# A three-stage transformer kernel: one order of two splits swapped, three pacing rates and the depth of a read changed

## The chip, the cores and the metric

The kernel runs on one core of one Trainium2 chip. The time is the device time of one launch in microseconds (us); the comparison is between medians of several launches of each kernel. One launch of each kernel is also recorded by the hardware profiler; all rows below come from that launch of the kernel before.

## What is computed

Two transformer blocks on 256 tokens of width 2048, all in float32. The first is a convolution and neighbourhood attention block with an MLP. The second has latent attention, a gated unit and, last, a retrieval layer over 16,384 experts. Only this last layer, and the second product of the MLP, lie near the change:

```python
f = jnp.square(jax.nn.relu(h @ w_up[l])) @ w_down[l]        # first block, the MLP

def peer_ffn(h, w_pq, peer_keys, peer_u, peer_v):            # second block, the last layer
    q = jnp.einsum("bsd,dhk->bshk", h, w_pq).reshape(B, S, PEER_HEADS, 2, KEY_DIM)
    sub = jnp.einsum("bshpk,hpnk->bshpn", q, peer_keys).astype(jnp.float32)
    s, i = lax.top_k(sub, PEER_TOPK)
    cand = (s[..., 0, :, None] + s[..., 1, None, :]).reshape(B, S, PEER_HEADS, PEER_TOPK * PEER_TOPK)
    ...
    top_s, pos = lax.top_k(cand, PEER_TOPK)
    idx = jnp.take_along_axis(cidx, pos, axis=-1)
    gate = jax.nn.softmax(top_s, axis=-1).astype(h.dtype)
    ...
        u = jnp.take(peer_u, i_blk, axis=0)
        a = jax.nn.gelu(jnp.einsum("td,thkd->thk", x_blk, u)) * g_blk
        v = jnp.take(peer_v, i_blk, axis=0)
        return jnp.einsum("thk,thkd->td", a, v)
```

Most tokens do not gather their experts. The kernel computes gelu(h @ peer_u.T) for all experts, multiplies it by a table that holds the gate of a chosen expert and zero elsewhere, and multiplies the result by peer_v. For 64 of the 256 tokens the table is not used: their rows of peer_u and peer_v are gathered, two experts of each of the 64 tokens per gather, 64 gathers of each matrix.

## The kernel before

**Weight steps.** All weights stream through three 1 MB buffers (`raw`), loaded on SP's queue (L209). Half a buffer is one weight step. For each step ScalarE writes the rounded high part (`whi`, L131), VectorE the rest (`wlo`, L132), and TensorE multiplies both by activations that have been split in the same way (L264). There are four `whi`/`wlo` pairs, so a split may run three steps ahead of its matmuls (`LOOK`). There are 1,124 weight steps, numbered from 0.

**Order.** `Builder.run` writes the program by hand, step by step: first `prep`, which splits the weights of a step up to three ahead, and which asks SP for the next load when it has used up a buffer; then `jit`, which splits the activations of a step two ahead where these are made just in time (the MLP's second product, and the value passes below); then the matmuls of the step; then `tick`. Each engine executes its own instructions in this written order.

**Side work.** `tick` moves generators forward. Each generator is a list of small portions of work and has a rate, the portions that it gets per weight step (`Gen`, `acc`). A generator that is not done when its result is needed is drained: the whole rest is written at once at that place.

**The last layer.** From step 612 on the passes are U(0), U(1), U(2), U(3), V(0), U(4), V(1), U(5), V(2), U(6), V(3), U(7), then V(4 to 7) in one piece of 128 steps; each other pass has 32 steps. A U pass multiplies by an eighth of peer_u; after every eight steps a `turn` transposes the result (L1635, L1637) and puts its gelu into a ring of four eighths (`s_ra`, `s_rc`). A V pass multiplies a ring entry by an eighth of peer_v; its stationary operand `s_vj` is split from the ring two steps ahead. Beside the passes run, one after the other:
- `top_gen` (*the search*): the second top 16, all on VectorE (L1485 to L1489, L1542 to L1547). It begins after the lists of the first top 16; rate 1.0.
- `g_gen` (*the gates*): 24 portions. Each makes one-hot tables on VectorE (four instructions, L1674 to L1677), multiplies them on TensorE (L1687), copies the product on ScalarE (L1689, two instructions) and stores 0.5 MB to the DRAM tile `scratch` (L1690). Two sets of tables are used in turn. Rate 0.5.
- `sparse` (*the gathers*): 128 gathers of 1 MB each on GpSimd's queue into three buffers (L1592), one instruction of VectorE for each (L1607 for peer_u, L1609 for peer_v). Rates 0.48 in U passes, 0.30 in V passes.
- `r_gen(e)` (*the reads*): once pass U(e) is done and all gates are made, three reads of 0.5 MB from `scratch` on SP's queue into one buffer (`s_g`, L1698); each is followed, some ticks later, by a multiplication of a part of ring entry e on VectorE (L1704). `jit_V` drains `r_gen(e)` before it splits from entry e.

In this kernel the search lasts from step 612 (the lists end at 625) to step 682, the gates to step 733, the gathers from there to step 1091. V(0) begins at step 740. The reads for entry 0 begin after step 733 and are drained at step 738.

The names TensorE (PE), VectorE (DVE), ScalarE (ACT), GpSimd (POOL) and SyncE (SP) are used below with the short forms that rows of the profile have.

Of the kernel before, what the change touches and what calls it, by code (L numbers as in the profile page):

```python
# [18 lines left out]
JLOOK = 2  # L19
# [38 lines left out]
class Builder:  # L58
# [22 lines left out]
    def H(self, i, key, dt=FT):  # L81

        s, n = (i // 2, 4096) if i >= 8 else (10 + i, 2048)
        if self.halves.get(s, (None,))[0] != key:
            self.halves[s] = key, self.pool.tile([128, n], dt, name=f"s{s}_{key}", tag=f"s{s}")
        o = 2048 * (i % 2) if i >= 8 else 0
        return self.halves[s][1][:, o:o + 2048]
# [197 lines left out]
    def run(self):  # L285
        prepared = jitted = 0
        while prepared < LOOK:
            self.first.upto(prepared + 1)
            self.prep(prepared)
            prepared += 1  # L290
        for i, halves, blocks, behind in self.order():
            p = self.pieces[i]
            self.spare = p.spare
            for need in p.need:
                g, n, hs = (need + (None,))[:3] if isinstance(need, tuple) else (need, None, None)
                if blocks in (None, (0,)) and (hs is None and halves[0] == 0 or hs in halves):
                    g().drain() if n is None else g().upto(n)
            while self.may_prep(prepared, i, behind):
                self.prep(prepared)
                prepared += 1  # L300
            while jitted <= i + JLOOK:
                self.jit(jitted)
                jitted += 1
            self.mm(i, halves, blocks)
            if p.lag is None:
                if p.post:
                    p.post(p)
                self.tick()
            else:
                self.tick(0.5 if blocks is None else 0.25)  # L310
                if p.post:
                    p.post(p, halves) if blocks is None else p.post(p, halves, blocks)
        for g in self.gens:
            g.drain()
# [622 lines left out]
XLOOK = 2  # L937
ASIDE = (1, 3, 4, 5, 6, 7)

GATE_RATE = 0.5  # L940

SPARSE_RATE = (0.48, 0.30)
CONV_RATE = [1.7, 1.2]
NA_RATE = [1.0, 1.0]
CONV_POOL = (2, 3, 6, 7)
# [2 lines left out]
def phase3(b, C, W, gs, X, ident, transposes, residual, norm_of, stat2, act_pair, lhs_of, res_need, bcast, jits,  # L948
# [429 lines left out]
    def fuse():  # L1378
        for c in range(0, 16, 4):
            yield  # L1380
            yield
            t = [v3(H(4 + k, "h", FR)[:, :], 16)[:, c:c + 4] for k in range(2)]
            A.activation(t[0][:, :, 64:128], t[1][:, :, 0:64], AF.Copy)
# [32 lines left out]
    def Qp(n, h):  # L1416
        return H(6, "top")[:, (n % 2) * 1024 + h * 512:(n % 2) * 1024 + h * 512 + 512]
# [10 lines left out]
    def key_gen(n):  # L1428
        if n:
            gs["key", n - 1].drain()  # L1430
        for _ in transposes(lambda h: Qp(n, h), 0, evac_to(lambda: qT(n))):
            yield
        yield
        for h in range(2):
            p = b.bank()
            for i in range(4):
                PE.matmul(p[:, i * 128:i * 128 + 128], qT(n)[:, i, h * 128:h * 128 + 128], keys()[:, 4 * n + i],
                          start=True, stop=True)
            A.activation(SUB(h)[:, n * 512:n * 512 + 512], p[:, :], AF.Copy)
            yield  # L1440
        if n == 3:
            for h in range(2):
                b.dbg(f"sub.{h}", SUB(h)[:, :])
# [5 lines left out]
    def post_pq(n):  # L1449
        def f(p):  # L1450
            if n == 0:
                for h in range(2):
                    gs["res3", h].drain()
                norm_of(r3, ss3)
                nc.gpsimd.dma_start(H(16, "k")[:, :], d["keysT"])
                for r, lo in ((rd, 0), (rsp, 64)):
                    for o in (0, 64):
                        nc.gpsimd.dma_start(r[o:o + 64, :], r3[lo:lo + 64, 1:2])
                nc.gpsimd.dma_start(fold, d["fold"])
            for h in range(2):  # L1460
                A.activation(Qp(n, h), b.ps[p.banks[h][0]][:, :], AF.Copy, scale=r3[:, h:h + 1])
            gs["key", n] = b.start(key_gen(n))
            gs["lists", n] = b.start(lists_gen(n))
            if n == 2:
                gs["fuse"] = b.start(fuse())
            if n == 3:
                gs["top"] = b.start(top_gen(), 1.0)
        return f

    for n in range(4):  # L1470
# [25 lines left out]
    def lists_gen(n):  # L1496
        V16, I16, _, rep = found()
        while not (gs["key", n].done and (n == 0 or gs["lists", n - 1].done)):
            yield
        for h in range(2):  # L1500
            for m in range(4 * n, 4 * n + 4):
                o = (h * 16 + m) * 16
                top16(V16[:, o:o + 16], I16[:, o:o + 16], SUB(h)[:, m * 128:m * 128 + 128], rep[m % 2][:, :128])
                yield

    def top_gen():
# [13 lines left out]
        for h in range(2):  # L1520
# [52 lines left out]
            yield  # L1573
        gs["G"] = b.start(g_gen(), GATE_RATE)

# [41 lines left out]
    def ring(e, h):  # L1617

        j = e % 4
        return v3(H(14 + j // 2, "rc")[:, j % 2 * 1024:j % 2 * 1024 + 1024] if h else H(10 + j, "ra")[:, :], 16)  # L1620
# [20 lines left out]
    def post_U(n):  # L1641

        def f(p):
            if n and ("s", n - 1) in gs:
                gs["s", n - 1].drain()
            for h in range(2):
                A.activation(GT(h), b.ps[p.banks[h][0]][:, :], AF.Copy, scale=rd if h else r3[:, 0:1])
            gs["s", n] = b.start(turn(n))
            if n % 4 == 3:
                gs["R", n // 4] = b.start(r_gen(n // 4))  # L1650
        return f
# [5 lines left out]
    def g_gen():  # L1657
# [12 lines left out]
        for k in range(25):  # L1670
# [8 lines left out]
            if k:  # L1679
# [10 lines left out]
                nc.gpsimd.dma_start(b.scratch[k], out[k % 2])  # L1690
        gs["sp"] = b.start(sparse(), SPARSE_RATE[0])

    def r_gen(e):
        while not (gs["s", 4 * e + 3].done and "G" in gs and gs["G"].done and (e == 0 or gs["R", e - 1].done)):
            yield
        t = H(7, "g")[:, 1024:2048]
        for j in range(3):
            nc.sync.dma_start(t.rearrange("p (k m) -> p k m", k=8),  # L1698
                              b.scratch[8 * j:8 * j + 8, :, 128 * e:128 * e + 128].rearrange("k p m -> p k m"))
            yield  # L1700
            yield
            yield
            R = ring(e, j // 2)[:, :, j % 2 * 64:j % 2 * 64 + 64].rearrange("p n (k t) -> p k n t", k=8)
            V.tensor_tensor(R, R, t.rearrange("p (k n t) -> p k n t", k=8, n=16), op=OP.mult)  # L1704
            yield
# [82 lines left out]
    def pace(i):  # L1788
        if "sp" in gs:
            gs["sp"].rate = SPARSE_RATE[i]  # L1790
        return Gen(iter(()))
# [131 lines left out]
```

## Time and profile before

| what | value |
|---|---|
| median of 3 launches | 3282.93 us (3282.73 to 3294.15) |
| the profiled launch's own time | 3288.91 us |
| its span, first to last instruction | 3287.1 us |
| busy: PE, DVE, ACT, POOL | 96%, 69%, 53%, 15% |
| moved by DMA | 768.52 MB, mean 234 GB/s |
| U and V passes (from step 612) | from 1903.8 us of the span |

A busy share is the share of the span in which the engine executed something. Busy time of PE is modelled at its ends, so small gaps do not show. The span is cut into stretches below by weight steps: a stretch begins where ACT begins the `whi` split of its first step.

### The profile page before, as it was taken

How to read it: one execution, taken by the hardware profiler on the slowest of the kernel's cores; microseconds unless marked ns; L12 is line 12 of the kernel's file. 1: busy time of each engine (PE TensorE's matmuls, PEld its weight loads, DVE VectorE, ACT ScalarE, POOL GpSimd, SP SyncE). 2: the span in 40 equal slices, each digit the busy share in tenths (PEclk: the TensorE clock that was granted, in tenths of full speed). 3: DMA queues.
4: the chain of work that ended last, by engine and by line, in shares of the span. 5: the costliest groups of instructions: out<-in, count | busy, mean ns of one | idle time of the engine just before them, and what ended most of it. 6: DMA issues, size and time to landing. Idle time of an engine off the chain costs nothing. (4 is left out here: it accounts for less than half of the span.)

```text
span 3287.1 us, 37918 instructions
## 1 busy us (share of the span) xinstructions
PE 3164.6 (96%) x14264; PEld 2474.4 (75%) x14264; DVE 2271.0 (69%) x2847; ACT 1725.9 (53%) x2490; POOL 480.5 (15%) x372
## 2 busy tenths in 40 slices
PE   8799999999999999999999999997899999999998
PEld 6577778888888788877778877775676767677776
DVE  6996554444555555654565599885898989898985
ACT  5666554444444455455544555675444545455554
POOL 3861010000000010000000100001131313232310
PEclk9999999999999999999999999998999999999999
DMA  6345455555555545544455555676999999999974
GB/s 224 134 163 182 179 178 180 179 179 181 191 189 183 200 139 214 181 160 144 140 184 189 180 183 201 240 266 231 339 397 350 400 351 397 346 400 359 365 296 154
DMA packets 135240, 768.52 MB, mean 234 GB/s; under 512 B 13008, under 2 KB 38016, under 8 KB 47568
## 3 DMA queue, kind: packets, MB, share of 16 engines
q1 hardware_dynamic: 110000, 604.81, 50.9%
q0 software_dynamic: 24768, 160.25, 12.4%
q8 instruction: 111, 1.82, 0.2%
q10 hardware_dynamic: 288, 1.05, 0.1%
q14 instruction: 73, 0.60, 0.1%
HBM read 750.82 MB, written 14.68 MB: 233 GB/s over the span
## 5 line engine op out<-in xcount | busy, mean ns | idle before, releaser
L132 DVE TENSOR_TENSOR wlo<-raw,whi 128x1024 fp32r<-128x1024 f32 (+2 forms) x1101 | 1350.9, 1235 | 790.5 <-ACT whi L131 780.9
L131 ACT ACTIVATE whi<-raw 128x1024 fp32r<-128x1024 f32 (+2 forms) x1113 | 1167.1, 1053 | 1050.4 <-PE ps L264 840.1
L264 PE MATMUL ps<-whi,s_x 128*128 128x512 f32 (+2 forms) x2816 | 908.6, 398 | 10.6 <-ACT whi L131 6.2
L264 PEld LDWEIGHTS ps<-whi,s_x 128*128 128x128 f32 x2816 | 533.0, 190 | 137.3 <-issue 8.3
L264 PE MATMUL ps<-whi,s_h 128*128 128x512 f32 x1760 | 604.6, 400 | 0.0
L264 PE MATMUL ps<-whi,s_vj 128*128 128x512 f32 x1536 | 542.7, 408 | 59.2 <-DVE s_vj L132 35.8
L264 PE MATMUL ps<-wlo,s_x 128*128 128x512 f32 (+2 forms) x1408 | 556.0, 395 | 16.3 <-DVE wlo L132 16.2
L264 PE MATMUL ps<-wlo,s_h 128*128 128x512 f32 (+1 forms) x1136 | 449.5, 396 | 6.2 <-DVE wlo L132 6.2
L264 PEld LDWEIGHTS ps<-whi,s_vj 128*128 128x128 f32 x1536 | 294.3, 193 | 170.9 <-DVE s_vj L132 48.0
L264 PE MATMUL ps<-wlo,s_vj 128*128 128x512 f32 (+1 forms) x1024 | 410.6, 401 | 0.0
L264 PEld LDWEIGHTS ps<-whi,s_h 128*128 128x128 f32 x1760 | 331.4, 188 | 99.9
L264 PEld LDWEIGHTS ps<-wlo,s_x 128*128 128x128 f32 x1408 | 267.9, 190 | 80.7 <-DVE wlo L132 24.3
L264 PE MATMUL ps<-whi,s_fj 128*128 128x512 f32 x1024 | 324.6, 397 | 2.8 <-DVE s_fj L132 2.0
L264 PEld LDWEIGHTS ps<-whi,s_fj 128*128 128x128 f32 x1024 | 193.5, 189 | 51.5 <-DVE s_fj L132 2.5
L264 PEld LDWEIGHTS ps<-wlo,s_h 128*128 128x128 f32 (+1 forms) x1136 | 185.9, 164 | 56.4 <-DVE wlo L132 10.4
L264 PE MATMUL ps<-wlo,s_fj 128*128 128x512 f32 x512 | 203.6, 398 | 0.0
L264 PEld LDWEIGHTS ps<-wlo,s_vj 128*128 128x128 f32 (+1 forms) x1024 | 168.5, 165 | 46.4 <-issue 1.0
L132 POOL TENSOR_TENSOR s_head<-raw,s_head 128x1024 fp32r<-128x1024 f32 x6 | 17.5, 2934 | 895.8 <-ACT s_head L131 895.8
L517 POOL TENSOR_TENSOR s_conv<-s_conv,s_u 128x256 f32<-128x256 f32 x120 | 122.6, 1054 | 44.1 <-ACT s_u L516 43.6
L1592 POOL DMA_INDIRECT s_k<-in_v_rows,vec x43 | 91.3, 2123 | 201.7 <-DVE s_sp L1609 179.7
L264 PEld LDWEIGHTS ps<-wlo,s_fj 128*128 128x128 f32 x512 | 96.8, 189 | 22.6
L1609 DVE SCALAR_TENSOR_TENSOR s_sp<-s_k,misc,s_sp 128x2048 f32<-128x2048 f32 x43 | 100.8, 2345 | 2.1 <-DMA s_k<-in_v_rows,vec 2.1
(333 smaller groups left out, 2972.9 us busy)
## 6 DMA issues: line engine op xcount, KB each, us to landing
raw<-in_peer_u SPq DMA_DIRECT2D x128, 1024.0 KB, 5.8
raw<-in_peer_v SPq DMA_DIRECT2D x128, 1024.0 KB, 7.0
raw<-in_w_in SPq DMA_DIRECT2D x101, 1024.0 KB, 4.8
raw<-in_w_up SPq DMA_DIRECT2D x64, 1024.0 KB, 4.8
raw<-in_w_down SPq DMA_DIRECT2D x64, 1024.0 KB, 4.8
raw<-in_w_out SPq DMA_DIRECT2D x32, 1024.0 KB, 4.8
raw<-in_w_pq SPq DMA_DIRECT2D x16, 1024.0 KB, 4.8
scratch<-s_k POOLq DMA_DIRECT2D x24, 512.0 KB, 2.9
```

Source lines behind the costliest of these rows:

```text
L131: nc.scalar.activation(hi, src, AF.Copy)
L132: (engine or nc.vector).tensor_tensor(lo, src, hi.bitcast(FT), op=OP.subtract)
L264: nc.tensor.matmul(self.ps[p.banks[h][b]][:xs[q].shape[-1], :w], xs[q], (wl if q == 1 else wh)[:, s], start=p.first and c == 0 and q == 0, ...
L517: G.tensor_tensor(o, o, t, op=OP.add)
L1592: nc.gpsimd.indirect_dma_start(buf[g % 3], None, d["v_rows" if g // 64 else "u_rows"], at)
L1609: V.scalar_tensor_tensor(Y(), t, a, Y(), op0=OP.mult, op1=OP.add)
```

## The change

Four edits. The generator rates of the search (1.0 to 1.3) and of the gates (0.5 to 0.8) are raised, those of the gathers lowered (0.48 to 0.45 and 0.30 to 0.28). In `r_gen` there are five ticks instead of three between a read and the multiplication that uses it, for all entries but the first. In `run`, `jit` comes before `prep`, in every step of the program that has both.

```diff
@@ Builder.run
+            while jitted <= i + JLOOK:
+                self.jit(jitted)
+                jitted += 1
             while self.may_prep(prepared, i, behind):
                 self.prep(prepared)
                 prepared += 1
-            while jitted <= i + JLOOK:
-                self.jit(jitted)
-                jitted += 1
             self.mm(i, halves, blocks)
...
-GATE_RATE = 0.5
-
-SPARSE_RATE = (0.48, 0.30)
+GATE_RATE = 0.8
+
+SPARSE_RATE = (0.45, 0.28)
...
@@ post_pq
             if n == 3:
-                gs["top"] = b.start(top_gen(), 1.0)
+                gs["top"] = b.start(top_gen(), 1.3)
...
@@ r_gen
             nc.sync.dma_start(t.rearrange("p (k m) -> p k m", k=8),
                               b.scratch[8 * j:8 * j + 8, :, 128 * e:128 * e + 128].rearrange("k p m -> p k m"))
-            yield
-            yield
-            yield
+            for _ in range(5 if e else 3):
+                yield
             R = ring(e, j // 2)[:, :, j % 2 * 64:j % 2 * 64 + 64].rearrange("p n (k t) -> p k n t", k=8)
```

In the changed program the search ends at step 668, the gates at step 701, and the gathers run from step 701 to step 1070. The reads for entry 0 take steps 702 to 714, those for entry 1 steps 715 to 732, for entry 2 steps 733 to 750, for entry 3 steps 751 to 768; none is drained. The changed program has one line less, so L1704 is L1703 there. Where the programs differ is shown by their instructions in written order, at three places.

VectorE while the gates are made, before (`wlo` is a weight step's split; the four lines after it are one portion of the gates):

```order
L132 TENSOR_TENSOR wlo_81<-raw_75,whi_77 128x1024
L132 TENSOR_TENSOR wlo_82<-raw_73,whi_78 128x1024
L1674 TENSOR_TENSOR s_k<-s_g 128x1024
L1675 TENSOR_TENSOR s_k<-s_g 128x1024
L1676 TENSOR_TENSOR s_k<-s_k,s_g 128x1024
L1677 TENSOR_TENSOR s_k<-s_k,s_g 128x1024
L132 TENSOR_TENSOR wlo_83<-raw_73,whi_79 128x1024
L132 TENSOR_TENSOR wlo_80<-raw_74,whi_76 128x1024
```

and now:

```order
L132 TENSOR_TENSOR wlo_81<-raw_73,whi_77 128x1024
L1674 TENSOR_TENSOR s_k<-s_g 128x1024
L1675 TENSOR_TENSOR s_k<-s_g 128x1024
L1676 TENSOR_TENSOR s_k<-s_k,s_g 128x1024
L1677 TENSOR_TENSOR s_k<-s_k,s_g 128x1024
L132 TENSOR_TENSOR wlo_82<-raw_74,whi_78 128x1024
L1674 TENSOR_TENSOR s_gb<-s_g 128x1024
L1675 TENSOR_TENSOR s_gb<-s_g 128x1024
L1676 TENSOR_TENSOR s_gb<-s_gb,s_g 128x1024
```

A portion stands in four of five weight steps instead of in every second one.

VectorE where the reads for entry 0 are used, before (L1704 multiplies a ring entry by a read, L1587 belongs to the gathers, `s_vj` is the stationary operand of V(0)):

```order
L1704 TENSOR_TENSOR s_ra<-s_ra,s_g 128x8x16x8
L1587 TENSOR_TENSOR s_sp<-s_x,s_sp 64x2048
L132 TENSOR_TENSOR wlo_81<-raw_74,whi_77 128x1024
L1704 TENSOR_TENSOR s_ra<-s_ra,s_g 128x8x16x8
L1704 TENSOR_TENSOR s_rc<-s_rc,s_g 128x8x16x8
L132 TENSOR_TENSOR s_vj<-s_ra,s_vj 128x256
L132 TENSOR_TENSOR s_vj<-s_rc,s_vj 128x2x64
```

and now:

```order
L1703 TENSOR_TENSOR s_ra<-s_ra,s_g 128x8x16x8
L1587 TENSOR_TENSOR s_sp<-s_x,s_sp 64x2048
L132 TENSOR_TENSOR wlo_81<-raw_73,whi_77 128x1024
L132 TENSOR_TENSOR wlo_82<-raw_74,whi_78 128x1024
L132 TENSOR_TENSOR wlo_83<-raw_74,whi_79 128x1024
L132 TENSOR_TENSOR wlo_80<-raw_75,whi_76 128x1024
L1703 TENSOR_TENSOR s_ra<-s_ra,s_g 128x8x16x8
L1607 ISA s_gb,misc<-s_gb,s_sp 128x2048
L1607 ISA misc 128x1
L132 TENSOR_TENSOR wlo_81<-raw_75,whi_77 128x1024
```

The three multiplications stand in U(3), weight splits lie between them, and no split of `s_vj` follows them.

VectorE in V(1), between the first and the second multiplication of entry 4, before:

```order
L1704 TENSOR_TENSOR s_ra<-s_ra,s_g 128x8x16x8
L132 TENSOR_TENSOR wlo_81<-raw_74,whi_77 128x1024
L132 TENSOR_TENSOR s_vj<-s_ra,s_vj 128x256
L132 TENSOR_TENSOR s_vj<-s_rc,s_vj 128x2x64
L132 TENSOR_TENSOR wlo_82<-raw_75,whi_78 128x1024
L132 TENSOR_TENSOR wlo_83<-raw_75,whi_79 128x1024
```

and now:

```order
L1703 TENSOR_TENSOR s_ra<-s_ra,s_g 128x8x16x8
L132 TENSOR_TENSOR s_vj<-s_ra,s_vj 128x256
L132 TENSOR_TENSOR s_vj<-s_rc,s_vj 128x2x64
L132 TENSOR_TENSOR wlo_83<-raw_75,whi_79 128x1024
L132 TENSOR_TENSOR wlo_80<-raw_73,whi_76 128x1024
```

The pair of `s_vj` splits stands ahead of the weight split of the same step, on ACT as on DVE.

## Rows read from the trace of the kernel before

**Rows 1.** Stretches: start:end and length, us; busy by engine; clock; DMA share, GB/s.

```profile
826.30:915.90 89.60, 89.60 (x386) 72.08 (x385) 48.81 (x49) 42.29 (x49) 0.00 (x0) 1.00 0.54 188
1903.80:2086.00 182.20, 179.01 (x826) 137.38 (x825) 172.91 (x376) 99.30 (x116) 0.00 (x0) 1.00 0.57 201
2111.00:2254.70 143.70, 143.70 (x938) 112.24 (x937) 117.69 (x138) 111.09 (x120) 14.39 (x26) 1.00 0.73 262
1903.80:2254.70 350.90, 347.71 (x1877) 268.92 (x1876) 308.44 (x537) 224.41 (x252) 15.99 (x29) 1.00 0.64 229
2254.70:2371.00 116.30, 85.48 (x339) 62.65 (x338) 79.36 (x95) 45.77 (x70) 19.93 (x12) 0.85 0.79 285
2371.00:2455.80 84.80, 81.77 (x367) 61.84 (x366) 74.91 (x70) 38.40 (x44) 23.65 (x15) 1.00 0.99 392
2455.80:2540.00 84.20, 77.35 (x320) 57.92 (x319) 74.31 (x92) 43.67 (x69) 17.71 (x11) 0.94 0.93 351
2540.00:2618.70 78.70, 78.70 (x358) 60.58 (x358) 72.29 (x68) 39.87 (x45) 23.55 (x14) 1.00 0.99 398
2618.70:2703.90 85.20, 78.55 (x333) 58.78 (x332) 74.35 (x91) 43.91 (x68) 17.74 (x11) 0.98 0.92 354
2782.60:2867.90 85.30, 79.14 (x336) 59.16 (x335) 75.25 (x82) 43.85 (x68) 23.12 (x11) 0.98 0.94 357
2948.10:3287.00 338.90, 318.04 (x1330) 235.88 (x1328) 267.98 (x310) 178.64 (x282) 65.71 (x31) 0.98 0.78 297
3067.70:3086.40 18.70, 18.70 (x81) 14.20 (x81) 16.55 (x20) 10.52 (x17) 3.45 (x3) 1.00 0.93 353
```

**Rows 2.** Waits in V(0), 2254.7 to 2371 us: total us, times, longest.

```profile
PE ps L264 <- ACT s_vj L131: 19.9, 1, 19.9
...
PE ps L264 <- DVE s_vj L132: 10.8, 5, 3.9
```

**Rows 3.** Timeline of DVE, start of V(0): start us, us, what, [idle before <-releaser].

```profile
2267.40 1.23 DVE L1704 TENSOR_TENSOR s_ra<-s_ra,s_g 128x1024 f32<-128x1024 f32 x1 [10.34 <-DMA s_g<-scratch]
...
2280.14 1.23 DVE L1704 TENSOR_TENSOR s_ra<-s_ra,s_g 128x1024 f32<-128x1024 f32 x1 [7.93 <-DMA s_g<-scratch]
2285.32 1.23 DVE L1704 TENSOR_TENSOR s_rc<-s_rc,s_g 128x1024 f32<-128x1024 f32 x1 [3.96 <-DMA s_g<-scratch]
```

**Rows 4.** Timeline in V(1), all engines, lines between left out.

```profile
2470.22 0.53 SPq L1698 DMA_DIRECT2D s_g<-scratch  x1
...
2483.29 1.23 DVE L1704 TENSOR_TENSOR s_ra<-s_ra,s_g 128x1024 f32<-128x1024 f32 x1 [2.35 <-DMA s_g<-scratch]
2484.43 1.22 DVE L132 TENSOR_TENSOR wlo<-raw,whi 128x1024 fp32r<-128x1024 f32 x1
2485.57 0.42 DVE L132 TENSOR_TENSOR s_vj<-s_ra,s_vj 128x256 fp32r<-128x256 f32 x1
...
2486.04 1.65 PE L264 MATMUL ps<-whi,s_vj 128*128 128x512 f32 x3 [3.88 <-DVE s_vj L132]
```

**Rows 5.** Waits of DVE ahead of L1704, 2371 to 3010 us: releaser, us, times.

```profile
  DMA s_g<-scratch: 25.2, 13
```

**Rows 6.** Reads of L1698, 2371 to 3010 us, from issue to landing.

```profile
DMA to landing us min/median/max: 6.5/8.3/13.0
```

**Rows 7.** Waits of PE, 2371 to 3287 us: total us, times, longest.

```profile
PE ps L264 <- DVE s_vj L132: 25.0, 15, 3.9
```

**Rows 8.** Groups by line, DVE, 1903.8 to 2086 us: count, busy us, mean ns, idle before.

```profile
L132 DVE TENSOR_TENSOR wlo<-raw,whi 128x1024 fp32r<-128x1024 f32 x69 | 83.6, 1212 | 5.1 <-ACT whi L131 5.0
```

**Rows 9.** Groups by line, DVE then ACT, 2111 to 2254.7 us.

```profile
L1674 DVE TENSOR_TENSOR s_gb<-s_g 128x1024 f16<-128x1024 f16 x11 | 7.6, 692 | 5.9 <-PE ps L1687 5.9
...
L1689 ACT ACTIVATE s_k<-ps 128x512 f32<-128x512 f32 x48 | 54.2, 1258 | 28.5 <-issue 16.4 <-PE ps L1687 12.1
L131 ACT ACTIVATE whi<-raw 128x1024 fp32r<-128x1024 f32 x48 | 50.4, 1077 | 2.4 <-PE ps L264 1.9
```

**Rows 10.** The page's groups by line: one gather's instruction on VectorE.

```profile
L1609 DVE SCALAR_TENSOR_TENSOR s_sp<-s_k,misc,s_sp 128x2048 f32<-128x2048 f32 x43 | 100.8, 2345 | 2.1 <-DMA s_k<-in_v_rows,vec 2.1
```

## The prediction

> **What bounds the kernel now.** I read the stretches first [rows 1], from step 612 to the end, and asked of each what TensorE would need alone. A pure stretch of eight weight steps took 18.70 us with PE busy throughout, so a step costs 2.34 us. A U pass without idle PE took 78.70 us for 32 steps and four turns; less 32 x 2.34 = 74.9 that leaves 3.8, or 1.0 us for a turn. The gate stretch is PE-bound too: 143.7 us for 48 steps (112.3), six turns (6) and 24 gate portions, hence 25.4 / 24 = 1.06 us each. Against these prices the stretches show where time is lost. V(0) took 116.3 us where 32 steps and a turn need 75.8: it lost 40 us. V(1) to V(3) took 84.2, 85.2 and 85.3 us, some 9 us too long each. U(4), right after V(0), took 84.8 against 78.9. The search stretch took 182.2 us for 70 steps and nine turns (172.8); there DVE was busy 172.9 us, so both engines need the same time and their interplay costs 5%.
>
> Then the waits of V(0) [rows 2]: PE stood 19.9 us at once for `s_vj`, then 10.8 us in five waits. The timeline [rows 3] tells why. The reads for entry 0 are drained, so each stands directly before its use, one after the other through one buffer: DVE waited 10.34, 7.93 and 3.96 us. The clock column shows what follows an idle PE: 0.85 of full speed over V(0), so part of the stretch ran at the lower level of 1.2 GHz, while undisturbed passes show 1.00.
>
> The later V passes have a smaller form of it [rows 4]. A read was issued at 2470.22; DVE came to its use 10.7 us later and waited 2.35 us more; behind it in DVE's order stood a weight split and only then the `s_vj` split, and PE waited 3.88 us. From 2371 to 3010 us 13 uses waited, 25.2 us in all [rows 5], since a read takes 6.5 to 13.0 us to land [rows 6]. PE waited 25.0 us for `s_vj` in the rest of the kernel [rows 7].
>
> **The change, part by part.** The sum is made against the profiled launch: 3288.9 us, of which 1.8 lie outside the span; the median is 6 us lower, and I carry the difference over to it.
>
> *Search at 1.3.* The same portions fall on 56 steps instead of 70, so DVE loses 14 weight splits of 1.21 us [rows 8]: 172.9 - 17 = 156 us, against 56 x 2.34 + 7 = 138 on PE. DVE becomes the sole bound. Its share of the stretch was 95% before, with two engines abreast; I take 96%: 163 us. Bounds: 156 if DVE never waits, 170 if it keeps 95% and PE's gaps cost some clock as well.
>
> *Gates at 0.8.* Steps 668 to 701, 33 of them with 24 portions and four turns. PE needs 33 x 2.34 + 4 + 24 x 1.06 = 107 us. DVE needs 33 x 1.21 + 24 x 4 x 0.69 [rows 9] = 106. ACT needs 33 x 1.08 + 24 x 2 x 1.13 = 90 and about 10 for the turns. Three engines abreast: with the 5% of the search stretch I get 112 us; bounds 107 and 122 (15%, if ACT's in-order copies make `whi` late).
>
> *The freed steps, 701 to 740.* These are 39 steps and five turns with gathers beside them: PE 96 us; DVE 39 splits, 15 gathers' instructions of 2.35 [rows 10], six multiplications of 1.23 and L1587, about 92. The DMA: 39 steps of 0.52 MB, 18 gathers of 1.05 MB, six reads of 0.52 MB make 42 MB. The busiest U pass moved 398 GB/s at a DMA share of 0.99 and still had no idle PE [rows 1]; at that rate 42 MB take 107 us. Three gathers (3.1 MB, 8 us) may run late without anybody waiting, so I take 101; bounds 96 and 107.
>
> The Trainium skill gives a core about 358 GB/s of HBM when its neighbour streams too ("DMA: Bandwidth & Descriptors", Specifications); by that the 42 MB would take 117 us and the stretch 16 more than I take. The 398 GB/s of the row speak against it on this launch.
>
> So steps 612 to 740 go from 350.9 us [rows 1] to 163 + 112 + 101 = 376: **25 us lost**.
>
> *V(0) without the drain.* The reads for entry 0 are over 26 steps earlier. What is late next: DVE, whose work in a V pass was 74.3 us in V(1), and in V(0) now has three multiplications more (3.7) and about one gather less (2.4): 75.7, abreast of PE's 75.8. With 5%: 79.5 us. Gain 36.8. U(4), which suffered from the tail of it, becomes a normal U pass of 79.5: gain 5.3. Bounds for the pair: 154 if all is hidden, 170 if V(0) stays like V(1).
>
> *Five ticks, and `jit` first.* Two steps more (4.7 us) between a read and its use cover every wait of rows 5, whose mean is 1.9 us. Where `s_vj` was late without a read, at the start of a pass's second half, it comes one weight split (1.22 us) earlier in DVE's order. The price: `wlo` of a step comes 0.7 us later on DVE in every second step; that split has three steps of lead, 7 us, and nobody else queues behind it. ACT waits for the same matmuls to release either buffer, so no new wait there. I expect V(1) to V(3) at 78 instead of 84.2 to 85.3: gain 20.7. Bounds 76 and 83.
>
> *The end, from 2948.1.* 338.9 us, with one pass's worth of late reads, and the gathers end 21 steps earlier. I take a gain of 6; bounds 0 and 10. SP's queue keeps its order of loads but for the reads, which now wait less; nobody waits there for more.
>
> *The MLP.* In its 32-step window PE was busy 89.60 of 89.60 us, with DVE at 48.81: the swap costs nothing, since DVE has 40 us to spare; if that were wrong, 0.7 us in every second step would be the price.
>
> *Sum.* +25 - 36.8 - 5.3 - 20.7 - 6 = -44 us. 3288.9 becomes 3245; the median 3282.9 becomes **3239 us**.
>
> **Rivals.**
>
> *The DMA takes the gain back.* If 398 GB/s were possible only with long runs of plain loads, and the gathers with the reads get the 351 GB/s of V(1), the freed steps take 42 MB / 351 = 120 us (+19) and reads land later by as much as the added ticks give, so that V passes stay at 84 (nothing of the 20.7) and V(0) gets 84 (4.5 less). -44 + 19 + 20.7 + 4.5 = 0: 3283 us. For it: DMA shares of 0.92 to 0.99 in all these passes. Against it: the U pass at 398 GB/s held 14 gathers. By the 358 GB/s of the Trainium skill ("DMA: Bandwidth & Descriptors", Specifications) the freed steps take 117 us, so that this rival's time would be 3280.
>
> *The search hides better.* If DVE runs without gaps at 156 us, gates take 107 and V passes reach 76, the net gain grows by 7 + 5 + 6 + 3 = 21: 3218 us. For it: a DVE that alone bounds a stretch has nobody to wait for.
>
> *Slower: the gates become a chain.* Each portion goes through tables on DVE (2.76 us), PE (1.06), the copy on ACT (2.26), then the next weight split on ACT (1.08) and DVE (1.21), 8.4 us in all [rows 9]. If at four portions in five steps the two sets of tables no longer overlap these, 24 portions take 201 us instead of 112, and the kernel gets 89 - 44 = 45 us slower: 3328. It decides from (112 + 44) / 24 = 6.5 us a portion on. For it: ACT already waited 28.5 us before the copies. Against it: those waits hid fully at a portion every two steps, and the sets allow two portions in flight, 4.2 us each.
>
> *The change does nothing at V(0)* would need a drain there; the written order excludes it.
>
> **How the numbers follow.** The forecast 0.62; better hiding 0.18; DMA 0.15; gate chain 0.05. A measurement of this kernel tells 0.5%, 16 us, from no change: the first two cases are faster by more but for the edge of the first, some 0.78; same 0.17; slower 0.05. The forecast's own bounds, not all at one end, give 3222 to 3262. The range must reach better hiding at 3218 and some less; at the top I stop short of the DMA case: 3212 to 3268.
>
> **What would show it.** Right: V(0) near 80 us with no DVE wait for `scratch` over 2 us, V(1) to V(3) below 80, PE's waits for `s_vj` below 8 us after 2371. Steps 612 to 740 near 376 us with DVE over 95% until the search ends. Wrong: that stretch over 395 us, idle PE behind `wlo` while the gates are made (the chain), or waits for `raw` and for reads in the freed steps (the DMA).

## The result and the profile after

The changed kernel takes 3239.22 us, the median of 4 launches (3238.02 to 3240.65). The kernel before, run beside it, takes 3284.9 (3282.73 to 3294.15). The ratio is 0.9855, with a 95% interval of 0.9844 to 0.9867: 46 us faster, where 44 were forecast. The profiled launch of the changed kernel took 3238.02 us with a span of 3236.3, so the two spans differ by 50.8 us.

The stretches after, cut at the same weight steps as [rows 1]. Columns as there: start:end and length, busy time by engine, granted clock, DMA share, GB/s. In order: steps 612 to 740 in one, then its three parts (search, gates, freed steps), V(0), U(4), V(1), V(2), V(3), and step 996 to the end.

```profile
1897.80:2283.90 386.10, 360.87 (x1898) 274.10 (x1897) 342.98 (x569) 222.87 (x253) 42.00 (x44) 0.99 0.70 256
1897.80:2055.90 158.10, 146.88 (x663) 110.44 (x661) 150.81 (x353) 79.20 (x94) 0.00 (x0) 0.99 0.50 179
2055.90:2163.20 107.30, 106.23 (x720) 82.11 (x719) 101.16 (x134) 84.06 (x92) 11.71 (x22) 1.00 0.76 271
2163.20:2283.90 120.70, 107.76 (x521) 81.54 (x519) 91.01 (x84) 59.62 (x69) 30.28 (x22) 0.97 0.90 342
2283.90:2364.50 80.60, 76.27 (x325) 57.15 (x324) 75.09 (x94) 43.10 (x69) 14.83 (x10) 0.98 0.99 384
2364.50:2440.40 75.90, 75.90 (x346) 58.38 (x345) 70.05 (x64) 39.20 (x46) 21.24 (x13) 1.00 0.98 396
2440.40:2516.40 76.00, 76.00 (x333) 58.00 (x332) 71.82 (x92) 43.64 (x69) 13.09 (x10) 1.00 0.99 380
2595.20:2674.40 79.20, 78.15 (x341) 59.10 (x340) 73.63 (x88) 44.13 (x69) 29.52 (x11) 1.00 0.97 365
2754.50:2828.30 73.80, 73.80 (x325) 56.33 (x324) 71.12 (x81) 44.96 (x69) 30.80 (x10) 1.00 0.98 378
2906.90:3236.30 329.40, 315.50 (x1339) 235.97 (x1338) 254.41 (x302) 183.58 (x282) 40.66 (x23) 0.99 0.75 280
```

Against the forecast, by stretch (us):

| stretch | before | forecast | after |
|---|---|---|---|
| search, 612 to 668 | | 163 | 158.1 |
| gates, 668 to 701 | | 112 | 107.3 |
| freed steps, 701 to 740 | | 101 (96 to 107) | **120.7** |
| 612 to 740 together | 350.9 | 376 | 386.1 |
| V(0) | 116.3 | 79.5 | 80.6 |
| U(4) | 84.8 | 79.5 | 75.9 |
| V(1), V(2), V(3) | 84.2, 85.2, 85.3 | 78 each | 76.0, 79.2, 73.8 |
| 996 to the end | 338.9 | 333 | 329.4 |
| end of the MLP, 352 to 384 | 101.6 | 101.6 | **96.4** |

The waits of PE after V(0), 2364.5 to 3236.3 us, as in [rows 7] (us in total, times, longest). Of 25.0 us for `s_vj` 0.8 are left:

```profile
PE ps L264 <- DVE s_vj L132: 0.8, 2, 0.6
```

The 25.2 us that DVE waited before the multiplications [rows 5] have no counterpart: from 2364 to 2960 us the 11 uses of line 1703 waited for no read. The reads themselves land no sooner than in [rows 6]; they are only asked for earlier:

```profile
DMA to landing us min/median/max: 7.8/8.8/11.7
```

So the total is right. The two entries in bold are not, and the experiments find a larger error that the table does not show: what the earlier gates are worth.

### The profile page after: what moved, and what is told of

Same layout as the page of the kernel before. It is cut to its first block, busy times and chain, and to the rows that moved or that the text cites. A ratio compares the mean times of both kernels' runs of the same rounds, so it can differ in the third digit from the quotient of the medians.

```text
span 3236.3 us, 38053 instructions
## 1 busy us (share of the span) xinstructions
PE 3147.2 (97%) x14264; PEld 2464.6 (76%) x14264; DVE 2268.5 (70%) x2847; ACT 1727.8 (53%) x2490; POOL 482.8 (15%) x372
## 4 chain that ended last, share of the span: by engine, by line
PE 80%; DVE 10%; issue 4%; DMA 3%; ACT 2%; POOL 0%; SPq 0%; POOLq 0%; DVEq 0%; ACTq 0%
PE ps L264 75%; DVE wlo L132 3%; DVE s_conv L521 3%; DMA raw<-in_peer_u 1%; PE ps L477 1%; DMA s_g<-scratch 1%; ACT whi L131 1%; PE ps L1262 1%; PE ps L1635 0%; PE ps L1261 0%; DVE s_x L727 0%; DMA raw<-in_peer_v 0%; PE ps L1637 0%; DMA raw<-in_w_in 0%; ACT s_k L1689 0%
## 5 line engine op out<-in xcount | busy, mean ns | idle before, releaser
L264 PE MATMUL ps<-whi,s_vj 128*128 128x512 f32 x1536 | 530.6, 400 | 4.0 <-DVE s_vj L132 2.8
L264 PE MATMUL ps<-wlo,s_vj 128*128 128x512 f32 (+1 forms) x1024 | 403.8, 394 | 0.5 <-DVE wlo L132 0.5
L1592 POOL DMA_INDIRECT s_k<-in_v_rows,vec x43 | 101.7, 2366 | 222.4 <-DVE s_sp L1609 195.0
```

Source lines behind the costliest of these rows:

```text
L264: nc.tensor.matmul(self.ps[p.banks[h][b]][:xs[q].shape[-1], :w], xs[q], (wl if q == 1 else wh)[:, s], start=p.first and c == 0 and q == 0, ...
L1592: nc.gpsimd.indirect_dma_start(buf[g % 3], None, d["v_rows" if g // 64 else "u_rows"], at)
```

## Experiments: which edit brings the gain

The theory of the prediction: the earlier gates bring most, 42 us at V(0) and U(4) for 25 lost in steps 612 to 740; the deeper reads and the swap bring the rest; the gathers' lower rate matters little. Two rivals: the moved work is paid in full where it now stands, so that the earlier gates are worth nothing; and the deeper reads alone bring the gain, with nothing left for the swap and the rates. All ratios below are to the kernel before, which ran beside each group of runs with medians of 3284.9 to 3288.4 us; so two absolute times from different groups compare to some 3 us.

**The swap alone**, on the kernel before.

```diff
-            while self.may_prep(prepared, i, behind):
-                self.prep(prepared)
-                prepared += 1
             while jitted <= i + JLOOK:
                 self.jit(jitted)
                 jitted += 1
+            while self.may_prep(prepared, i, behind):
+                self.prep(prepared)
+                prepared += 1
```

> The kernel before with the order of jit and prep swapped, nothing else. In the changed kernel three things improved that could come from the swap: PE's waits for s_vj (25.0 us after 2371 us before, 2.8 us after), and, not foreseen, 5 us at the end of the MLP (steps 352 to 384 took 101.6 us before, 96.4 after). Theory: the swap takes the s_vj waits without a late read (about 8 us) and the 5 us of the MLP, V(0) keeps its drain: about 13 us less than the kernel before, near 3271. Rival: the MLP's 5 us are a chance of one launch and s_vj was late through the reads alone: within 4 us of the kernel before.

Measured: 3282.75 us (3275.97 to 3288.75), ratio 0.9988 (0.9978 to 0.9998), about 4 us. PE's waits for `s_vj` did not fall; from the end of V(0) (2367.2 us) on, where [rows 7] have 25.0, they were:

```profile
PE ps L264 <- DVE s_vj L132: 25.5, 13, 4.0
```

While the read was late, the order of the two splits behind it made no difference: both stand behind the waiting multiplication. Of the profiled launch's 3.4 us in span, 5.3 come from the end of the MLP (96.3 us for 101.6), and V(1) got longer (87.0 for 84.2).

**Five ticks alone**, for all entries but the first, on the kernel before.

```diff
-            yield
-            yield
-            yield
+            for _ in range(5 if e else 3):
+                yield
```

> The kernel before with five ticks instead of three for entries 1 to 7, nothing else. Theory: two more steps cover the waits for reads after V(0), each of V(1) to V(3) loses 6 to 8 us and the end some: 3262; V(0) keeps its drain. Rival: at the old rates of the gathers the DMA is too full, the ticks alone bring what the swap alone brought, some 4 us, and only the edits together bring more: 3280.

Measured: 3261.32 us (3260.11 to 3262.61), ratio 0.992 (0.9904 to 0.9937), about 26 us: more than half of the whole change from one loop. From 2370 to 3000 us DVE's waits before the multiplications fell from 25.2 us [rows 5] to

```profile
  DMA s_g<-scratch: 4.1, 4
```

and PE's waits for `s_vj` to the end from 25.0 [rows 7] to

```profile
PE ps L264 <- DVE s_vj L132: 11.8, 10, 2.9
```

Of the gain 14 us lie in V(1) to V(3) (240.8 for 254.7), 4 at the end, and 10 in V(0) (106.2 for 116.3), although its drain stays. DVE's waits before the multiplications in V(0), before and with five ticks:

```profile
  DMA s_g<-scratch: 32.0, 7
```

```profile
  DMA s_g<-scratch: 21.7, 3
```

The three that are left are the drained reads of [rows 3]. The other four, 9.8 us, were later reads, late for want of ticks as in V(1).

**All the rates alone**, with three ticks and the old order.

```diff
-GATE_RATE = 0.5
+GATE_RATE = 0.8
-SPARSE_RATE = (0.48, 0.30)
+SPARSE_RATE = (0.45, 0.28)
-                gs["top"] = b.start(top_gen(), 1.0)
+                gs["top"] = b.start(top_gen(), 1.3)
```

> The kernel before with the new rates of search, gates and gathers; three ticks for all reads, prep ahead of jit. Theory: V(0) loses its drain (-36) and U(4) its tail (-9), steps 612 to 740 cost the same 35 us more as in the changed kernel, V(1) to V(3) keep their late reads: about -10, near 3275. Rival: with fewer gathers beside a V pass the reads land in time without more ticks, and the rates alone bring most of it: near 3250.

Measured: 3280.08 us (3273.5 to 3286.19), ratio 0.9982 (0.997 to 0.9993), about 6 us. Here V(0) is free of the drain and takes 84.4 us, and yet almost nothing is won: steps 612 to 740 take 395.5 (158.1 + 109.9 + 127.5) where they took 350.9. The waits from 2160 to 2450 us show that the reads are as late as ever:

```profile
DVE s_ra L1704 <- DMA s_g<-scratch: 28.6, 8, 11.2
PE ps L264 <- DVE wlo L132: 16.9, 7, 8.1
```

**All but the swap**: the changed kernel with `prep` ahead of `jit` again.

```diff
             while self.may_prep(prepared, i, behind):
                 self.prep(prepared)
                 prepared += 1
+            while jitted <= i + JLOOK:
+                self.jit(jitted)
+                jitted += 1
```

> The changed kernel with prep ahead of jit again (rates and ticks new). Theory: ticks take the late reads of V(1) to V(3) and the last stretch (some 15 us of the rates' result), the swap is still worth 8 to 13 us: near 3250, and the 5 us at the end of the MLP are lost again. Rival: with reads in time the swap has nothing left to do: 3239, as the changed kernel.

Measured: 3247.9 us (3244.85 to 3251.81), ratio 0.9885 (0.9868 to 0.9901). With the rates in place the ticks are worth 32 us (3280.08 to 3247.9), and with rates and ticks in place the swap is worth 9. Some 4 of these are the end of the MLP (100.3 us without the swap, 96.4 with it). For the rest, no multiplication waits for a read here after 2360 us, and yet PE's waits from 2280 us to the end hold

```profile
PE ps L264 <- DVE s_vj L132: 8.0, 6, 3.5
```

that is, `s_vj` behind a weight split. The swap removes it, as forecast, but only once no read is late.

**The earlier gates taken back**: the changed kernel with search and gates at their old rates. Ticks, swap and the gathers' lower rates stay; the drain at V(0) is back, and the gathers end at the last step but one instead of step 1070.

```diff
-GATE_RATE = 0.8
+GATE_RATE = 0.5
-                gs["top"] = b.start(top_gen(), 1.3)
+                gs["top"] = b.start(top_gen(), 1.0)
```

> The changed kernel with search and gates back at 1.0 and 0.5: five ticks, jit first and the lower gather rates stay, the drain at V(0) is back, the gathers end at the last step but one. By the stages of the two profiles the earlier gates gave 44.6 us in V(0) and U(4) and cost 35.2 in steps 612 to 740, so they are worth 9 us: 3249, if the late end of the gathers costs nothing. Rival: by the shares forecast before the result (42 less 25) they are worth 17, and the late gathers cost 5 to 10 more at the end: 3262.

Measured: 3237.88 us (3235.97 to 3241.21), ratio 0.985 (0.9834 to 0.9867), the same as the changed kernel and less than either expectation. The stretches of this kernel (612 to 740, V(0), U(4), then all from 612 to 996):

```profile
1898.10:2249.00 350.90, 347.70 (x1877) 268.88 (x1876) 308.43 (x537) 224.31 (x252) 16.09 (x29) 1.00 0.64 230
2249.00:2350.10 101.10, 80.69 (x340) 60.15 (x339) 74.48 (x90) 45.45 (x70) 16.77 (x11) 0.90 0.84 308
2350.10:2437.70 87.60, 81.55 (x360) 61.67 (x359) 77.80 (x72) 39.02 (x45) 20.57 (x14) 0.98 0.99 386
...
1898.10:2907.00 1008.90, 975.52 (x4638) 745.97 (x4637) 891.17 (x1133) 557.32 (x704) 177.75 (x123) 0.99 0.85 321
```

and 612 to 996 of the changed kernel:

```profile
1897.80:2906.90 1009.10, 977.69 (x4629) 745.09 (x4628) 918.71 (x1147) 556.09 (x703) 217.79 (x137) 0.99 0.87 336
```

Against this kernel the changed one loses 35.2 us in steps 612 to 740 and gains 32.2 in V(0) and U(4) (188.7 to 156.5); 612 to 996 takes 1008.9 and 1009.1 us. The drain is there and costs a wait of PE of 16.9 us at one point in V(0), but to avoid it costs as much:

```profile
PE ps L264 <- ACT s_vj L131: 16.9, 1, 16.9
```

That the gathers end some 50 steps sooner buys nothing either: 996 to the end takes 328.9 us here and 329.4 in the changed kernel.

## Experiments: the freed steps

Steps 701 to 740 took 120.7 us instead of 101. Two things in their profile could be the cause. The waits of this stretch in the changed kernel:

```profile
ACT whi L131 <- DMA raw<-in_peer_u: 36.0, 12, 4.9
DVE s_ra L1703 <- DMA s_g<-scratch: 15.5, 3, 10.6
PE ps L264 <- DVE wlo L132: 10.2, 4, 7.6
```

and its timeline around the largest of them (start, duration, what, idle before and its releaser):

```profile
2183.16 0.38 SPq L1698 DMA_DIRECT2D s_g<-scratch  x1
...
2198.08 1.23 DVE L1703 TENSOR_TENSOR s_ra<-s_ra,s_g 128x1024 f32<-128x1024 f32 x1 [10.61 <-DMA s_g<-scratch]
...
2202.94 0.79 PE L264 MATMUL ps<-wlo,s_h 128*128 128x512 f32 x1 [7.59 <-DVE wlo L132]
```

The read is issued at 2183.16 and used at 2198.08, 14.9 us later. Entry 0 still has three ticks between the two, and DVE was at the use 4.3 us after the issue. DVE works in order: it stands 10.61 us, the weight splits behind it are late, and PE stands 7.59 us. Behind this wait PE is slower as well: from 2203 to 2210 us the granted clock is 0.68. That is the first cause. The 36.0 us that ACT waits for `raw` are the second: the weight loads themselves are late, beside gathers and reads.

**Five ticks for the first entry too.**

```diff
-            for _ in range(5 if e else 3):
+            for _ in range(5):
                 yield
```

> The changed kernel with five ticks for the reads of entry 0 as well. In the changed kernel DVE waits 10.6 us for the first read of entry 0 and PE stands 7.6 us behind it, in steps 701 to 740, which took 120.7 us where 101 were forecast. Theory: the short ticks are half of that excess, and two more steps take 5 us off DVE's wait: 3233. Rival: the three first gathers and the loads fill the DMA there, weights are as late as the read, and the wait only moves to raw: 3239.

Measured: 3236.44 us (3231.1 to 3244.96), ratio 0.985 (0.9826 to 0.9873). The stretch became 9.7 us shorter, and PE's wait for `wlo` in it fell from 10.2 to 3.6 us; ACT's for `raw` did not:

```profile
2166.40:2277.40 111.00, 104.13 (x499) 78.41 (x499) 87.61 (x81) 59.11 (x69) 29.34 (x22) 0.98 0.95 363
...
ACT whi L131 <- DMA raw<-in_peer_u: 36.3, 12, 6.5
...
PE ps L264 <- DVE wlo L132: 3.6, 5, 1.1
```

The total hardly moved: U(4), V(3) and U(7) took 3.2, 4.7 and 4.3 us more in the profiled launch. Over the whole run ACT waited 141.6 us for `raw` of peer_u and 106.8 of peer_v, where it waited 129.2 and 86.4 in the changed kernel. This reads as if steps that come faster met a DMA that is full; it is one launch, and was not tested by itself.

**Three gathers instead of 128.** The rest is left out (VectorE multiplies what lies in the buffers, so that its work stays).

```diff
-            nc.gpsimd.indirect_dma_start(buf[g % 3], None, d["v_rows" if g // 64 else "u_rows"], at)
+            if g < 3:
+                nc.gpsimd.indirect_dma_start(buf[g % 3], None, d["u_rows"], at)
...
-                V.tensor_tensor_reduce(t, t, xs, 1.0, 0.0, OP.mult, OP.add, a)
+                V.tensor_tensor_reduce(Y(), t, xs, 1.0, 0.0, OP.mult, OP.add, a)
```

> The changed kernel with 3 of the 128 gathers; all their instructions on VectorE stay, working on the first three gathers' rows, and those for peer_u write to another tile. Left out: the other 125 MB, so the 64 gathered tokens' results are not computed. Theory: the DMA makes steps 701 to 740 long (120.7 us where PE needs 96): without the gathers that stretch takes some 105 (the first three are still there beside the first read), waits for raw fall from 216 to below 30 us, the U passes lie at their 78.9. Rival: DVE's work sets the stretch, which stays above 115.

Measured, one launch: 3224.45 us, 14.8 less than the changed kernel's median. The freed steps, V(0), U(4) and V(1):

```profile
2163.90:2276.30 112.40, 103.01 (x499) 78.76 (x497) 89.00 (x83) 60.47 (x69) 10.13 (x10) 0.95 0.78 271
2276.30:2352.90 76.60, 76.28 (x334) 57.96 (x333) 74.76 (x92) 45.47 (x68) 0.00 (x0) 1.00 0.76 260
2352.90:2431.60 78.70, 78.70 (x357) 60.58 (x357) 71.88 (x69) 40.30 (x46) 0.00 (x0) 1.00 0.61 214
2431.60:2507.60 76.00, 76.00 (x334) 58.02 (x333) 71.96 (x90) 45.58 (x69) 0.00 (x0) 1.00 0.67 237
```

and the waits from step 701 to the end:

```profile
DVE s_ra L1704 <- DMA s_g<-scratch: 13.7, 2, 10.1
ACT whi L131 <- DMA raw<-in_peer_u: 9.8, 4, 3.2
PE ps L264 <- DVE wlo L132: 7.5, 2, 7.0
```

(One line was added, so line 1704 is the change's 1703.) Without the gathers' traffic the freed steps are 8.3 us shorter, and ACT waits 9.8 us for peer_u over all that follows instead of 36.0 in this stretch alone. The late first read stays: DVE 10.1 us, PE 7.0. So the two causes are separate; if their shares add, the stretch without either would take 120.7 - 9.7 - 8.3 = 102.7 us, near the 101 of the forecast. Both at once was not run. The passes come out at 76 to 79 us, which is what the prices of [rows 1] gave for PE alone.

**Gathers at their old rates**, the rest as changed.

```diff
-SPARSE_RATE = (0.45, 0.28)
+SPARSE_RATE = (0.48, 0.30)
```

> The changed kernel with the gathers back at 0.48 and 0.30; they end at step 1040 instead of 1070. Theory: U and V passes have a DMA share of 0.97 to 1.00 already, 6% more gathers in them make weights and reads late: passes 1 to 2 us longer each, 5 to 10 us in all, half of it won back after step 1040: near 3244. Rival: the rates of the gathers do nothing either way: 3239.

Measured: 3251.48 us (3248.86 to 3253.48), ratio 0.9894 (0.9873 to 0.9914): 12 us of the gain hang on this small step, which the prediction did not price at all. ACT's waits from V(0) to the end, with the old rates and then as changed:

```profile
ACT whi L131 <- DMA raw<-in_peer_u: 111.4, 45, 5.6
ACT whi L131 <- DMA raw<-in_peer_v: 96.2, 43, 6.4
```

```profile
ACT whi L131 <- DMA raw<-in_peer_u: 90.0, 42, 4.8
ACT whi L131 <- DMA raw<-in_peer_v: 86.4, 42, 4.4
```

The largest parts are U(4) (81.6 us for 75.9), the freed steps (124.0 for 120.7), V(3) and U(5) (3.4 and 3.2 more).

## Experiments: a better pace

Is the search too fast, or the gates? **Search at 1.0**, the rest as changed:

```diff
-                gs["top"] = b.start(top_gen(), 1.3)
+                gs["top"] = b.start(top_gen(), 1.0)
```

> The changed kernel with the search back at 1.0: it ends at step 682, the gates at 715, the gathers at 1093, the reads for entry 0 still before V(0). Theory: at 1.3 DVE alone bounds the search (158 us for 56 steps where PE needs 138), at 1.0 both engines need the same and the loss is 8; so steps 612 to 740 take some 181 + 107 + 78 = 366 us instead of 386, of which 3 to 5 come back in later passes with more gathers: 3222. Rival: what bounds these steps is the sum of all work put ahead of V(0), and the excess moves into the shorter freed stretch and V(0): 3235 to 3240.

Measured: 3233.92 us (3230.03 to 3241.64), ratio 0.9848 (0.9823 to 0.9873). Steps 612 to 740 took 369.5 us, 16.6 less; steps 612 to 668 take 144.4 as in the kernel before. U(4) and V(3) gave back 10.7 of it. The gain over the changed kernel is not certain by the intervals.

**Gates at 0.5**, the rest as changed:

```diff
-GATE_RATE = 0.8
+GATE_RATE = 0.5
```

> The changed kernel with the gates back at 0.5: they end at step 719, the reads for entry 0 at 732, so there is still no drain. Theory: gates at 0.5 are bound by PE at 2.99 us a step, so 51 steps take 152 us, and the 21 freed steps 65: with the search's 158 some 375 instead of 386, and the gathers, 18 steps later, cost a few us at the end: near 3232. Rival: the gates at 0.8 already ran at PE's floor (107.3 us where PE needs 107), so nothing is to be had there, and gathers that end at step 1099 cost more than they give: 3245.

Measured: 3243.8 us (3238.55 to 3246.35), ratio 0.9865 (0.9843 to 0.9887). Steps 668 to 701, now with fewer portions in them, took 97.4 us instead of 107.3, steps 701 to 740 no less (121.1 for 120.7); V(0), U(4) and U(6) took 3.1, 7.3 and 4.2 us more. No gain.

**Search at 1.0 and five ticks for all entries**, the two edits that helped their stretch:

```diff
-            for _ in range(5 if e else 3):
+            for _ in range(5):
...
-                gs["top"] = b.start(top_gen(), 1.3)
+                gs["top"] = b.start(top_gen(), 1.0)
```

> The changed kernel with the search at 1.0 and five ticks for entry 0 too. In the run with five ticks for all reads steps 701 to 740 went from 120.7 to 111.0 us, but the time hardly moved, since later passes got longer by as much, with more waits for raw. Theory: the two edits add up in steps 612 to 740 (some 356 us), half of the ticks' part comes back later: 3217. Rival: the DMA sets the time from step 701 on, so the ticks give nothing more: as with the search alone.

Measured: 3227.2 us (3224.91 to 3233.52), ratio 0.9823 (0.98 to 0.9846): the best found, clearly ahead of the kernel before and some 0.3% ahead of the change, though the two ratios' intervals just touch (0.9846 and 0.9844). The two edits did not add up where they stand: steps 612 to 740 took 369.1 us, where the search at 1.0 alone had 369.5 and 356 were expected. V(0) took 79.2 us, where it had 82.7. Against the search at 1.0 alone (3233.92) the intervals do not tell a gain. ACT's waits for `raw` over the whole run were 102.2 and 82.7 us, less than the change's 129.2 and 86.4.

**The same with gathers at 0.40 in U passes and 0.30 in V passes:**

```diff
-SPARSE_RATE = (0.45, 0.28)
+SPARSE_RATE = (0.40, 0.30)
```

> The best so far (search at 1.0, gates at 0.8, five ticks for all reads, jit first) with the gathers at 0.40 in U passes and 0.30 in V passes instead of 0.45 and 0.28. Theory: U passes have a DMA share of 1, V passes and the last pass have room, so gathers are moved to where they disturb less: 3222 against 3227. Rival: V passes are as full on DVE (1.21 + 0.35 + 0.30 x 2.35 = 2.27 us a step of 2.34) and lose what the U passes gain: 3227.

Measured: 3231.76 us (3223.55 to 3236.1), ratio 0.9826 (0.9806 to 0.9846). No difference that can be told; ACT's waits were 124.8 and 112.4 us. What is left of the DMA's cost does not go away when gathers are moved from the U passes to the V passes.

## Why the prediction was right or wrong

**The total: right, partly by luck.** The forecast summed the stretches, and most of them came out within 5 us, errors in both directions. Steps 612 to 740 cost 10 us more than forecast (386.1 for 376: the freed steps 20 more, search and gates 10 less); U(4), the V passes, the end and the end of the MLP gave some 17 more, V(0) one less. That these errors cancelled to within 7 us is luck, and so is it that the shares of the edits, which were wrong, add up to the right sum.

**Search: right.** DVE was busy 150.81 of 158.10 us, a share of 95.4% where 96% was taken; its work was 5 us less than worked out. The rival "hides better" wanted a DVE without gaps, and that did not come. Two other terms of that rival did: gates at 107, V(1) to V(3) at 76 on average (76.3). What kept its total of 3218 away are the freed steps and V(0).

**Gates: right, and the slower rival refuted.** 107.3 us with PE busy for 106.23: the stretch is bound by PE, at the lower bound of the forecast (107). No chain through tables, product and copy shows; it would have taken 201 us.

**V(0): right as to its time.** DVE busy 75.09 us (75.7 forecast), the pass 80.6 (79.5). Of the 35.7 us gained 26.5 are idle time of PE (30.8 before, 4.3 after); the other 9.2 are PE's own busy time for the same steps (85.48 and 76.27 us), at a granted clock of 0.85 before and 0.98 after. What the prediction had wrong is which edit this gain belongs to (below). **V(1) to V(3): right**, 229.0 us together for 234.

**The freed steps: wrong.** The step that failed is "three gathers may run late without anybody waiting, so I take 101", with 107 as the upper bound (107 less the 8 us of three gathers is 99; the other 2 us are not explained). The bound counted megabytes at 398 GB/s and PE's work, and left two waits out. The first read of entry 0 keeps its three ticks; the prediction said of entry 0 that its reads are "over 26 steps earlier" and asked what was late next in V(0), but not in the place where they now stand. That wait is worth 9.7 us. And 342 GB/s at a DMA share of 0.90 passed there, not 398; without gathers the stretch is 8.3 us shorter. To this extent the rival "the DMA takes the gain back" is true: it gave 120 us for this stretch, and the sign named for it came, waits for `raw` (36.0 us) and for reads (15.5 us) in the freed steps; but of the 19.7 us over the forecast 9.7 are the late first read, which that rival did not have. Its second half is false, since the V passes that follow ran at 365 to 380 GB/s and took 73.8 to 79.2 us, not 84. PE, too, had more to do in the freed steps than the 96 us counted: some 60 of the gates' 384 matmuls (L1687) fall behind the cut at step 701, 4.2 us in all. The Trainium skill's figure of 358 GB/s for a core whose neighbour streams too ("DMA: Bandwidth & Descriptors", Specifications) is not a limit of this launch on one core: U(4) moved 396 GB/s without idle PE.

**The earlier gates: the size of each end about right, the net wrong.** "25 us lost" against 42 won made them worth 17. With all else equal they are worth nothing: 35.2 lost, 32.2 won, and the totals are the same (3237.88 and 3239.22). The two errors behind it are the freed steps, above, and V(0) with the drain, which the forecast compared in its old state: with swap, ticks and slower gathers alone V(0) already falls from 116.3 to 101.1 us. It put all of the 40 us lost in V(0) down to the drained reads; 9.8 of the 32.0 us that DVE waited there belonged to later reads, which the ticks take away with the drain in place. The rows suggest why such a move is not free. Before, PE was busy 347.7 of 350.9 us in steps 612 to 740 [rows 1], with search, gates and gathers mixed in a way that left no engine as sole bound but PE. Now each part has a bound of its own: DVE in the search (150.8 us), PE in the gates (106.2), the DMA in the freed steps (0.90 of 120.7, 108.6). These three sum to 366 us, 18 more than PE's 347.7, before any gap. That reading is argued from the rows, and was not tested by itself.

**Five ticks: mechanism right, weight too small.** The forecast gave ticks and swap together 20.7 us, with a share of the end's 6. The ticks alone are worth 26, 10 of them in V(0), where the forecast gave them nothing, and 32 when the rates are in place.

**The swap: right where reads are on time, and wrong in the MLP.** "The swap costs nothing" there; it gained 5 us. The last section shows why.

**The gathers' rates: not priced.** They were mentioned only for ending 21 steps sooner. Lower by 6%, they bring 12 us, with the DMA at 0.97 to 0.99 in those passes and ACT's waits for late weight loads 31 us shorter (207.6 to 176.4).

The single edits on the kernel before sum to 36 us (4, 26, 6), all together bring 46 to 48: the swap counts only where the reads are on time, and the gathers' lower rate alone is worth 12 in the changed kernel, where all rates alone gave 6 in the kernel before. So of the two rivals the first holds (the earlier gates are worth nothing), and the second does not: the deeper reads bring the largest part, 26 to 32 us, but not all.

## What to carry to other kernels

A transfer that an in-order engine waits for stalls everything written behind it: ask for it early enough for its landing time under load, for its first use as well as for the steady state, before any order behind it is tuned. Work moved out of a stall gains only if the stretch that takes it in has room on every engine and on the DMA; add up that stretch's new bound, and test the move with all other edits kept. Where a change sets several rates at once, vary each by itself: here one that looked like a side effect was worth 12 us, and one that looked like the purpose was worth nothing.

## What was not expected: a small VectorE split beside GpSimd

At the end of the MLP both kernels make `s_head`, the early split of the next stage's first weight steps, partly on GpSimd. `s_fj` below is the activation operand of the MLP's second product, which `jit` splits. Steps 352 to 384, before and after:

```profile
1089.50:1191.10 101.60, 94.36 (x409) 74.76 (x408) 61.20 (x88) 54.77 (x101) 17.62 (x9) 0.97 0.41 144
```

```profile
1088.10:1184.50 96.40, 92.37 (x408) 73.86 (x407) 57.77 (x86) 54.23 (x101) 18.26 (x9) 0.98 0.44 151
```

The timeline of the kernel before at the place of the difference:

```profile
1140.09 5.42 POOL L132 TENSOR_TENSOR s_head<-raw,s_head 128x1024 fp32r<-128x1024 f32 x2 [691.18 <-ACT s_head L131]
1140.55 2.72 DVE L132 TENSOR_TENSOR s_fj<-s_f,s_fj 128x512 fp32r<-128x512 f32 x1
1143.20 3.39 DVE L132 TENSOR_TENSOR s_head<-raw,s_head 128x1024 fp32r<-128x1024 f32 x1
1143.33 1.22 PE L264 MATMUL ps<-whi,s_fj 128*128 128x512 f32 x2 [2.02 <-DVE s_fj L132]
```

and after:

```profile
1135.54 0.68 DVE L132 TENSOR_TENSOR s_fj<-s_f,s_fj 128x512 fp32r<-128x512 f32 x1
...
1139.15 6.03 POOL L132 TENSOR_TENSOR s_head<-raw,s_head 128x1024 fp32r<-128x1024 f32 x2 [691.60 <-ACT s_head L131]
1140.04 2.86 DVE L132 TENSOR_TENSOR s_head<-raw,s_head 128x1024 fp32r<-128x1024 f32 x1 [0.48 <-ACT s_head L131]
```

The split of `s_fj` takes DVE 0.68 us. Before, it began 0.46 us after GpSimd's first of two instructions of 2.7 us each, and ended 0.5 us after that one: 2.72 us. PE waited 2.02 us for it, and behind the wait ran at a lower clock: the granted clock from 1140 to 1152 us is 0.72, where it is 1.00 in the same 12 us after (1139 to 1151). With `jit` first the split is over before GpSimd begins, and what is slow then (2.86 us for 1.22) is a split that PE does not wait for at once. The swap alone shows 0.68 us at this place too and 96.3 us for the stretch; without the swap it is 2.72 and 100.3. It is so in every kernel of this document: the four with `prep` first have 2.72 or 2.73 us there and 100 to 102 us for the stretch, the ten with `jit` first 0.68 or 0.69 us and 96 to 98. The Trainium skill ("SBUF — State Buffer", SBUF: two separate sides) says that VectorE with two SBUF inputs and a GpSimd instruction that reads SBUF share a pair of ports, and that this is "an **exclusive lock**, not a bandwidth split" for a whole instruction: these rows agree. They have the form and no more, as spans on GpSimd are rough, and no run here moved the GpSimd split alone.

The prediction looked only at the 32-step window of the MLP in which PE was busy throughout, and took it for the whole. What the end of a stage runs beside its last steps has to be read by itself.
